# Mixed outputs of a hybrid encoder layer kept in two parts in HBM, their loads and those of w_out in a new order

## The chip, the cores and the metric

One core of one Trainium2 chip. The metric is the device time of one execution in microseconds (us). The times below are the median of three runs and one execution that was profiled.

## What is computed

One layer of a streaming encoder for 2048 prompt frames and 8 running streams of 16 frames. In the kernel these 2176 rows are 17 tiles of 128: tile 0 is the sample rows, tiles 1 to 16 are the prompt.

```
h = rms_norm(x, norm1_g);  p = h @ w_in                    # 1024 -> 3328
y_rw = rwkv7_mix(p[:, :1792])                              # 8 heads: chunked linear recurrence, group norm, gate
q, k, v = diff_project(p[:, 1792:])                        # rms norm and rope
o = softmax(q1 k1) v - lam * softmax(q2 k2) v              # chunk-causal; the samples with their cache
y_df = rms_norm(o, df_subln_g) * (1 - lam_init)
x = x + concat([y_rw, y_df]) @ w_out                       # the mixed outputs y: 1024 -> 1024
u = rms_norm(x, norm2_g) @ w_up                            # 1024 -> 5632
c = causal_dwconv(concat([conv_prev, u]), conv_w, conv_b)  # 3 taps
gate, up = split(c);  x = x + (silu(gate) * up) @ w_down   # 2816 -> 1024
```

Also written out are k, v, the last projected row, the recurrence's state and the last two rows of u. All is float32 to float32's precision: an operand is split into a high part rounded to the TensorE type (ACT copy, float32r) and a low part (DVE, value minus high), and a product is three matmuls: high x high, high x low, low x high.

## The kernel before, in words

The program is ordered by a planner (`Schedule`): every step of work is a Python generator (a stream) with a priority (0 is first); the planner has a model of each engine's time and always lets the stream go on whose operands it believes ready first and whose priority is lowest in number. What a stream issues goes, in that order, into the queues of the five engines, and each engine works its queue in order. All DMAs go through one queue, that of SP, which waits in order for what a transfer needs. `yield sd.has(...)` holds a stream until keys are done, `yield Slot(pool, tag)` until a buffer of a ring is free. Memory is handed out by hand (`Memory`, `Pool`), PSUM in 8 banks.

Three stages overlap at their edges. `phase_1`: q, k, v and the attention of the prompt; `subln` norms one pair of heads of a tile, turns it with TensorE and stores it in `scr["yt"]`, [feature / 128, 128, rows] float32 in HBM. `phase_2`: the rest of the projection (`project`, six blocks of tiles, each with 14 weight pieces that later blocks load from `s_wr`), the operands of the recurrence (`prep`, `prep2`). Beside what follows run `solver` (small triangular systems, DVE mostly), `chain` (the recurrence, tile by tile, each ended by `chain_out`, which norms, gates, turns and stores the other half of y), `samples` and `decode`.

`phase_3` works four blocks of four prompt tiles; the last has tile 0 too. It is set up when the key "projected" is done. Per block b: `inputs(b)` loads the block's mixed outputs Y: eight pieces of 128 x 512 go through a staging ring C of two buffers (shared with the convolutions), ACT makes the high part and DVE the low one in the tiles `hhi` and `hlo`. For b > 0 it waits for the keys ("up", b-1) and the last convolutions of block b-1; `hhi` and `hlo` are the very tiles that hold that block's normed h2, which the up units read. `out(b)` multiplies by w_out: a first half of 512 columns over four accumulators, then a second; `accumulate` adds each to the residual x (DVE), which frees the bank; `residuals` loads x only when the second stage is through (key "left"). `norm2` makes h2. Then 22 `up_unit`s (weights j and j + 22, the last one is unit 43), with five `down` groups between them (after j = 4, 8, 12, 16, 21), each two halves of columns; then `out(b+1)`, then the sixth `down` group. The key ("up", b) is set after the fifth group.

`order` lists the weight pieces in the order of use. The first time that a piece is used, `fetch` loads it raw (512 KB, ring `raw3` of two), `split` makes its two parts in the ring `w3` of four, and `keep` stores the parts (1 MB, `s_w3`, in the profile `s_w`); later blocks load the parts (1 MB). `weights` is allowed three pieces ahead of the one in use. The eight pieces of w_out have the numbers 66 to 73.

All instructions are recorded in one helper (L379 in the profile), so rows are told apart by operand names and shapes; tiles in SBUF are all named memory, PSUM is banks, `s_...` is scratch in HBM, `in_...` an input.

Of the kernel before, what the change touches and what calls it, by code (L numbers as in the profile page):

```python
# [462 lines left out]
class Kernel:  # L463
# [135 lines left out]
    def phase_1(self, scr, attention, scoring, projection):  # L599
# [376 lines left out]
        def values():  # L976

            q = 0
            for n in range(64):
# [12 lines left out]
                if h == 1:  # L992
                    yield
                    o = self.t(tp, [128, 256], "oB")
                    self.let(po)
                    for x in range(2):
                        nc.scalar.activation(o[:, x * 128:x * 128 + 128], po[:, x * 128:x * 128 + 128], AF.Identity, scale=rc.pop((p, i, x))[:, 0:1])
                    sd.add(self.subln(tp, mp, px, o, scr["yt"][4 + 2 * p:6 + 2 * p, :, (i + 1) * 128:(i + 2) * 128], "px"), 1, ("subln", p, i))
# [43 lines left out]
    def subln(self, tp, mp, pxt, o, dst, ptag):  # L1042
# [19 lines left out]
        yield  # L1062
        self.let(pt)
        yo = self.t(tp, [128, w], "sqB")
        nc.scalar.activation(yo, pt[:, :w], AF.Copy)
        yield
        nc.sync.dma_start(dst.rearrange("k p t -> p k t"), yo.rearrange("p (k t) -> p k t", k=H))


    def phase_2(self, scr, ctx, projection, early):  # L1070
# [3 lines left out]
        hp, xp, wr, wp = P("h2", 2), P("x2", 1), P("raw2", 2), P("w2", 3)  # L1074
# [119 lines left out]
        def weights():  # L1194
            for gi in range(nb * 14):
# [5 lines left out]
                if gi == 14:  # L1201
                    yield sd.has("scored", ("unit2", 13))
                    early.close()
                    sd.done.add("early")
# [462 lines left out]
    def chain_out(self, i, y, tiles, pools, tp, dst):  # L1667
# [44 lines left out]
        yo = self.t(t1, [128, 4, 128], "W")  # L1712
        nc.scalar.activation(yo, pt.rearrange("p (k t) -> p k t", k=4), AF.Copy)
        self.let(pt)
        yield
        nc.sync.dma_start(dst.rearrange("k p t -> p k t"), yo)
        yield "stored"

    def chain(self, scr, P, px):
# [13 lines left out]
        for i in range(1, NTILE):  # L1733
# [32 lines left out]
            yield from self.chain_out(i, y, tiles, pools, tp, scr["yt"][0:4, :, i * 128:i * 128 + 128])  # L1766
# [6 lines left out]
    def samples(self, scr, P, px):  # L1773
# [73 lines left out]
        yield from self.chain_out(0, y, tiles, pools, tp, scr["yt"][0:4, :, 0:128])  # L1847
        sd.done.add("samples")

    def decode(self, scr, P, px):  # L1850
# [118 lines left out]
        for x in range(2):  # L1969
            oh = self.t(tp, [128, 256], "oh")  # L1970
            nc.vector.tensor_copy(oh, o[:, x * 256:x * 256 + 256])
            yield from self.subln(lp, mp, px, oh, scr["yt"][4 + 2 * x:6 + 2 * x, :, 0:128], "px")
# [4 lines left out]
    def phase_3(self, scr, ctx):  # L1977
# [6 lines left out]
        wr = self.pools(rctx, True)("raw3", 2)  # L1984
# [47 lines left out]
        parts, made, used, known = {}, set(), [0], set()  # L2032
        first = [known.isdisjoint((x,)) and not known.add(x) for _, x in order]
# [12 lines left out]
        def fetch():  # L2046
            for i, (src, _) in enumerate(order):
# [9 lines left out]
        def weights():  # L2057
            for i in range(len(order)):
# [38 lines left out]
        def inputs(b):  # L2097
# [5 lines left out]
            if b:  # L2103
                yield sd.has(("up", b - 1), ("c", b - 1, 21), ("c", b - 1, 43))
            Y = [self.t(hp, [128, KT, NT], t, F32R, 128, KT * 640) for t in ("hhi", "hlo")]
            for k in range(KT):
                yield Slot(up, "C")
                raw = self.h(up, [128, NT], "C", room=640)
                runs = [(0, tiles[0], 4)] + ([(512, 0, 1)] if 0 in tiles else [])
                for o, i, n in runs:  # L2110
                    nc.sync.dma_start(raw[:, o:o + n * 128], yt[k, :, i * 128:(i + n) * 128])

                def done(k=k):
                    st["y"][k] = (Y[0][:, k], Y[1][:, k])

                sd.add(split(raw, Y[0][:, k], Y[1][:, k], done), 1)
            yield lambda: all(st["y"])
# [206 lines left out]
        def main():  # L2324
            yield from out(0)
            for b in range(nb):
# [17 lines left out]
        def all_inputs():  # L2344
            for b in range(nb):
# [9 lines left out]
    def run(self, scr):  # L2355
# [3 lines left out]
        with ExitStack() as ctx, ExitStack() as right, ExitStack() as left, ExitStack() as projection, ExitStack() as early:  # L2359
# [63 lines left out]
def lay_out(inputs):  # L2423
# [37 lines left out]
           "t": (NTILE, 4, 8, 32, 32), "yt": (KT, 128, NTILE * 128), "os": (128, 512), "xt": (NTILE, 128, D),  # L2461
# [43 lines left out]
```

## Time and profile before

| | us |
|---|---|
| time, median of 3 (lowest, highest) | 3441.08 (3439.51, 3445.29) |
| the profiled execution's own time | 3451.01 |
| its span, first to last instruction | 3448.8 |
| TensorE (PE) busy in the span | 3302.8 |
| VectorE (DVE) busy | 1977.7 |
| ScalarE (ACT) busy | 1391.5 |
| GpSimd (POOL) busy | 730.5 |
| HBM traffic, read and written | 514.00 MB, 181.09 MB |

How to read it: PE is the engine of the matmuls, PEld its weight loads, which overlap them. A row of a timeline gives start, duration, engine, operation, destination<-source, count, and in brackets the idle time of the engine just before and what ended it. Neighbouring instructions of a kind are merged in one row. SPq is the queue through which transfers are issued; its durations are the issuing, not the transfer. The granted clock (PEclk) is 1.00 at 2.4 GHz and 0.50 at 1.2 GHz.

### The profile page before, as it was taken

The numbers are of one execution on the slowest core, as the hardware profiler recorded it, in microseconds if no ns is written. First come the engines' busy times: TensorE is split into PE (matmuls) and PEld (weight loads), VectorE is DVE, ScalarE is ACT, GpSimd is POOL, SyncE is SP. The second block draws the span as 40 slices with busy tenths as digits, with TensorE's granted clock in tenths as the row PEclk, the third lists the DMA queues.
The fourth block names the chain that finished last, engine by engine and source line by source line (L and its number), as shares of the span: only waits on it lengthen the run. The fifth ranks groups of instructions, "written<-read, shape, count | busy, mean of one in ns | idle before, by whom it ended". The sixth has DMA issues, their size and how long they took to land.

```text
span 3448.8 us, 60191 instructions
## 1 busy us (share of the span) xinstructions
PE 3302.8 (96%) x23596; PEld 2753.1 (80%) x23596; DVE 1977.7 (57%) x3338; ACT 1391.5 (40%) x2837; POOL 730.5 (21%) x1700
## 2 busy tenths in 40 slices
PE   7999999988999997999999999999999999999999
PEld 6888788877888885777777777776667887899998
DVE  5787677786685657896664545435333333333334
ACT  5676566674444543434442322223232122222221
POOL 4433243333223321122211112131000000000000
PEclk9999999999999998999999999999999999999999
DMA  5433243178877777787785755657785565544443
GB/s 187 133 99 93 83 117 88 44 246 305 266 264 262 247 266 271 232 276 284 275 313 193 254 182 186 229 185 262 255 286 196 192 226 189 176 154 151 147 149 143
DMA packets 311099, 699.02 MB, mean 203 GB/s; under 512 B 124800, under 2 KB 198400, under 8 KB 260000
## 3 DMA queue, kind: packets, MB, share of 16 engines
q1 hardware_dynamic: 310816, 695.18, 59.1%
q8 instruction: 186, 3.05, 0.4%
q14 instruction: 97, 0.79, 0.1%
HBM read 514.00 MB, written 181.09 MB: 202 GB/s over the span
## 4 chain that ended last, share of the span: by engine, by line
PE 73%; DVE 11%; DMA 7%; issue 3%; POOL 2%; ACT 2%; SPq 1%; DVEq 0%; POOLq 0%; ACTq 0%
PE banks L379 73%; DVE memory L379 11%; POOL memory L379 2%; ACT memory L379 2%; SPq L379 1%; DMA memory<-s_xt 1%; DMA memory<-s_ar 1%; DMA memory<-s_yt 1%; DMA memory<-in_cv 0%; DMA s_wr<-memory 0%; DMA memory<-s_a 0%; DMA memory<-in_w_down 0%; DMA memory<-o_kp 0%; DMA s_tm<-memory 0%; DMA memory<-s_tm 0%
## 5 line engine op out<-in xcount | busy, mean ns | idle before, releaser
L379 PE MATMUL banks<-memory 128*128 128x512 f32 (+11 forms) x18952 | 2572.3, 309 | 64.4 <-ACT memory L379 31.1
L379 PEld LDWEIGHTS banks<-memory 128*128 128x128 f32 (+4 forms) x18824 | 2081.3, 164 | 446.4 <-issue 135.0
L379 ACT ACTIVATE memory<-banks 128x512 f32<-128x512 f32 (+8 forms) x1199 | 515.4, 442 | 1251.9 <-PE banks L379 1053.9
L379 DVE SCALAR_TENSOR_TENSOR memory<-memory 128x512 f32<-128x512 f32 (+7 forms) x830 | 605.0, 757 | 483.2 <-ACT memory L379 420.4
L379 ACT ACTIVATE memory<-memory 128x512 f32<-128x512 f32 (+11 forms) x921 | 618.3, 692 | 605.6 <-DVE memory L379 328.1
L379 PE MATMUL banks<-memory,memory 128*128 128x512 f32 (+3 forms) x3156 | 735.3, 368 | 10.2 <-DVE memory L379 5.0
L379 PEld LDWEIGHTS banks<-memory,memory 128*128 128x128 f32 (+1 forms) x3156 | 530.2, 188 | 117.1 <-DVE memory L379 12.4
L379 POOL COPY memory<-memory 128x2 f32<-128x2 f32 (+4 forms) x640 | 151.1, 261 | 1537.1 <-ACT memory L379 1500.7
L379 DVE TENSOR_TENSOR memory<-memory,memory 128x1024 fp32r<-128x1024 f32 (+6 forms) x289 | 280.7, 978 | 153.8 <-ACT memory L379 152.2
L379 DVE TENSOR_TENSOR memory<-memory 128x256 f32<-128x256 f32 (+18 forms) x501 | 290.1, 582 | 87.7 <-POOL memory L379 71.9
L379 DVE TENSOR_TENSOR memory<-memory,banks 128x512 f32<-128x512 f32 x238 | 162.1, 686 | 252.2 <-PE banks L379 250.9
L379 PE MATMUL banks<-ident,memory 128*128 128x128 f32 x1488 | 231.8, 282 | 67.3 <-DVE memory L379 32.5
L379 PEld LDWEIGHTS banks<-ident,memory 128*128 128x128 f32 x1488 | 177.3, 144 | 108.6 <-DVE memory L379 35.5
L379 POOL TENSOR_TENSOR memory<-memory 128x64 f32<-128x64 f32 (+6 forms) x453 | 216.1, 491 | 200.5 <-ACT memory L379 101.4
L379 DVE TENSOR_TENSOR memory<-banks,memory 128x256 f32<-128x256 f32 (+4 forms) x274 | 129.0, 471 | 209.2 <-PE banks L379 153.8
L379 ACT ACTIVATE memory<-banks,memory 128x128 f32<-128x128 f32 (+7 forms) x308 | 213.0, 706 | 85.2 <-DVE memory L379 56.2
L379 POOL TENSOR_TENSOR memory<-memory,mexp 128x4 f32<-128x4 f32 (+4 forms) x177 | 187.6, 1060 | 128.4 <-DVE memory L379 115.7
L379 DVE TENSOR_REDUCE memory<-banks 128x1 f32<-128x1024 f32 (+7 forms) x192 | 172.5, 908 | 36.1 <-PE banks L379 35.5
L379 DVE TENSOR_REDUCE memory<-memory 128x4 f32<-128x256 f32 (+24 forms) x314 | 145.1, 466 | 58.4 <-ACT memory L379 52.7
L379 POOL TENSOR_SCALAR memory<-memory 128x4 f32<-128x4 f32 (+4 forms) x159 | 44.3, 279 | 624.6 <-DVE memory L379 341.3
L379 ACT ACTIVATE memory<-banks,pvec 128x384 f32<-128x384 f32 (+1 forms) x98 | 49.3, 518 | 83.1 <-PE banks L379 77.6
L379 DVE SCALAR_TENSOR_TENSOR memory<-banks,memory,memory 128x384 f32<-128x384 f32 (+1 forms) x98 | 52.4, 537 | 52.6 <-ACT memory L379 50.6
(40 smaller groups left out, 465.8 us busy)
## 6 DMA issues: line engine op xcount, KB each, us to landing
memory<-s_w SPq DMA_DIRECT2D x222, 1024.0 KB
s_w<-memory SPq DMA_DIRECT2D x74, 1024.0 KB
memory<-s_wr SPq DMA_DIRECT2D x70, 1024.0 KB
memory<-in_w_up SPq DMA_DIRECT2D x44, 512.0 KB
memory<-s_xt SPq DMA_DIRECT2D x34, 512.0 KB
s_a<-memory SPq DMA_DIRECT2D x68, 256.0 KB
memory<-s_a SPq DMA_DIRECT2D x17, 1024.0 KB
memory<-in_x_prompt SPq DMA_DIRECT2D x32, 512.0 KB
```

The source lines that it names most:

```text
L379: r = f(*a, **k)
```

## The change

It does five things.

1. `scr["yt"]` gets a leading dimension of two: `subln` and `chain_out` (through the new `mixed`) make the high part with the ACT pass that they had, then a low part with a DVE subtraction from PSUM, and store both, with two DMAs.
2. `inputs` loads both parts straight into `hhi` and `hlo`, two 128-feature groups to a DMA, without ring C and without passes on ACT and DVE.
3. For b > 0 it waits for ("up", b-1) alone, and that key is set after the last up unit, ahead of the fifth `down` group.
4. `phase_3` is set up before "projected" is waited for; its weights, inputs and main part wait for that key themselves, but `fetch` already starts when five of the six blocks of the projection are done. Its raw ring is three deep and lies elsewhere; the second stage's raw ring is closed earlier.
5. w_out's pieces are loaded raw and split in the first two blocks, and stored in the second instead of the first.

```
-        hp, xp, wr, wp = P("h2", 2), P("x2", 1), P("raw2", 2), P("w2", 3)
+        hp, xp, wp = P("h2", 2), P("x2", 1), P("w2", 3)
+        rctx = ExitStack()
+        wr = self.pools(rctx, True)("raw2", 2)          # closed with early.close(), ahead of unit 14
...
+    def mixed(self, dst, p, hi, lo):
+        nc = self.nc
+        nc.scalar.activation(hi.bitcast(F32R), p, AF.Copy)
+        yield hi
+        nc.vector.tensor_tensor(out=lo.bitcast(F32R), in0=p, in1=hi, op=ALU.subtract)
+        yield lo
+        for x, part in enumerate((hi, lo)):
+            nc.sync.dma_start(dst[x].rearrange("k p t -> p k t"), part.rearrange("p (k t) -> p k t", t=128))
...
-        wr = self.pools(rctx, True)("raw3", 2)
+        wr = self.pools(rctx)("raw3", 3)
...
+        times = [sum(y == x for _, y in order[:i]) for i, (_, x) in enumerate(order)]
+        keeps = [n == (x >= 66) for n, (_, x) in zip(times, order)]
+        first = [n <= (x >= 66) for n, (_, x) in zip(times, order)]
...
         def fetch():
+            yield sd.has(("proj2", 4))
...
         def weights():
+            yield sd.has("projected")
...
-                    sd.add(keep(order[i][1], w), 1)
+                    if keeps[i]:
+                        sd.add(keep(order[i][1], w), 1)
...
             if b:
-                yield sd.has(("up", b - 1), ("c", b - 1, 21), ("c", b - 1, 43))
+                yield sd.has(("up", b - 1))
             Y = [self.t(hp, [128, KT, NT], t, F32R, 128, KT * 640) for t in ("hhi", "hlo")]
-            for k in range(KT):
-                yield Slot(up, "C")
-                raw = self.h(up, [128, NT], "C", room=640)
...
+            for k in range(0, KT, 2):
+                for x in range(2):
+                    for o, i, n in runs:
+                        nc.sync.dma_start(Y[x][:, k:k + 2, o:o + n * 128].bitcast(F32), yt[x, k:k + 2, :, i * 128:(i + n) * 128].rearrange("k p t -> p k t"))
+                for q in (k, k + 1):
+                    st["y"][q] = (Y[0][:, q], Y[1][:, q])
+                yield []
...
                     yield from up_unit(b, j)
+                    if j == 21:
+                        sd.done.add(("up", b))
                     if j in late(b):
                         yield from down(b, late(b)[j])
-                sd.done.add(("up", b))
...
+            self.phase_3(scr, ctx)
             sd.run(["projected"])
             projection.close()
             self.shut(self.middle[-1][1])
-            self.phase_3(scr, ctx)
```

## Rows read from the trace of the kernel before

**Rows 1.** The page: the span, and the busy time of each engine with its share of the span and its instructions.

```profile
span 3448.8 us, 60191 instructions
PE 3302.8 (96%) x23596; PEld 2753.1 (80%) x23596; DVE 1977.7 (57%) x3338; ACT 1391.5 (40%) x2837; POOL 730.5 (21%) x1700
```

**Rows 2.** The chain of waits that ended last, in order of time (start, duration, what): its pieces at the starts of blocks 1, 2 and 3.

```profile
1843.44 5.19 DMA memory<-s_yt
...
2387.84 7.40 DMA memory<-s_yt
...
2891.23 4.96 DMA memory<-s_yt
```

**Rows 3.** TensorE's timeline from 1316 to 1397 us, the start of block 0; the last row is out(0)'s last.

```profile
1324.25 0.79 PE L379 MATMUL banks<-memory 128*128 128x512 f32 x1 [8.34 <-ACT memory L379]
...
1330.67 3.62 PE L379 MATMUL banks<-memory 64*64 64x128 f32 x28
...
1337.97 0.43 PE L379 MATMUL banks<-memory 64*64 64x128 f32 x4 [3.35 <-ACT memory L379]
...
1339.68 6.36 PE L379 MATMUL banks<-memory 64*64 64x128 f32 x24 [1.28 <-DVE memory L379]
...
1346.30 4.08 PE L379 MATMUL banks<-memory 64*64 64x128 f32 x30
...
1359.36 1.22 PE L379 MATMUL banks<-memory 128*128 128x512 f32 x2 [2.52 <-ACT memory L379]
...
1366.46 21.73 PE L379 MATMUL banks<-memory 128*128 128x512 f32 x88 [5.87 <-DVE memory L379]
...
1394.57 2.33 PE L379 MATMUL banks<-memory 128*128 128x512 f32 x9
```

**Rows 4.** Windows of 10 us there: length, busy time (instructions) of PE, PEld, DVE, ACT and POOL, then the granted clock, the DMA engines' busy share, and GB/s.

```profile
1320.00:1330.00 10.00, 5.29 (x17) 4.00 (x18) 4.34 (x7) 2.12 (x2) 0.00 (x0) 0.57 0.53 131
...
1340.00:1350.00 10.00, 10.00 (x57) 7.62 (x49) 9.52 (x23) 3.21 (x6) 0.00 (x0) 0.71 1.02 414
...
1360.00:1370.00 10.00, 4.13 (x11) 2.82 (x10) 9.53 (x10) 1.06 (x1) 0.00 (x0) 0.52 1.00 383
```

**Rows 5.** TensorE's timeline at the starts of blocks 1, 2 and 3.

```profile
1847.87 1.11 PE L379 MATMUL banks<-ident,memory 128*128 128x128 f32 x4 [4.87 <-POOL memory L379]
...
2388.86 2.76 PE L379 MATMUL banks<-memory 128*128 128x64 f32 x18 [1.47 <-DVE memory L379]
...
2395.95 10.63 PE L379 MATMUL banks<-memory 128*128 128x512 f32 x80 [4.33 <-ACT memory L379]
...
2878.99 11.36 PE L379 MATMUL banks<-memory,memory 128*128 128x512 f32 x48
...
2897.07 43.28 PE L379 MATMUL banks<-memory 128*128 128x512 f32 x179 [6.71 <-ACT memory L379]
```

**Rows 6.** Windows of 5 us at these three places, columns as in rows 4.

```profile
1850.00:1855.00 5.00, 5.00 (x15) 3.93 (x14) 1.40 (x3) 1.44 (x3) 0.00 (x0) 0.57 0.54 157
...
2375.00:2380.00 5.00, 5.00 (x30) 3.23 (x32) 4.48 (x8) 1.19 (x3) 0.00 (x0) 1.00 1.00 365
...
2395.00:2400.00 5.00, 4.05 (x9) 2.77 (x9) 1.32 (x3) 1.88 (x3) 0.00 (x0) 0.50 0.38 122
...
2895.00:2900.00 5.00, 2.93 (x7) 2.19 (x8) 1.64 (x2) 1.48 (x2) 0.00 (x0) 0.54 0.50 164
...
2900.00:2905.00 5.00, 5.00 (x19) 4.01 (x18) 1.65 (x2) 1.48 (x2) 0.00 (x0) 0.78 0.48 138
```

**Rows 7.** The timeline of SP's queue: at the start of block 0, at one store of a mixed output (the fourth of chain_out after 1312, tile 8), and ahead of block 3.

```profile
1312.78 1.82 SPq L379 DMA_DIRECT2D memory<-s_yt  x2
...
1314.64 0.91 SPq L379 DMA_DIRECT2D memory<-in_w_out  x2
...
1316.54 13.79 SPq L379 DMA_DIRECT2D memory<-s_a  x16
...
1332.26 0.91 SPq L379 DMA_DIRECT2D s_w<-memory  x2
...
1357.28 3.10 SPq L379 DMA_DIRECT2D memory<-in_x_prompt  x4
...
1714.97 0.38 SPq L379 DMA_DIRECT2D s_yt<-memory  x1
...
2868.30 22.41 SPq L379 DMA_DIRECT2D memory<-s_w  x5
```

**Rows 8.** The timeline of ACT and DVE at the start of block 0: the first split of a w_out piece, the first split of a Y piece that had waited, and the first residual add.

```profile
1323.14 1.06 ACT L379 ACTIVATE memory<-memory 128x1024 fp32r<-128x1024 f32 x1 [4.74 <-DMA memory<-in_w_out]
...
1324.23 1.23 DVE L379 TENSOR_TENSOR memory<-memory,memory 128x1024 fp32r<-128x1024 f32 x1 [3.11 <-ACT memory L379]
...
1335.37 0.63 ACT L379 ACTIVATE memory<-memory 128x512 fp32r<-128x512 f32 x1 [9.82 <-DMA memory<-s_yt]
...
1336.03 0.69 DVE L379 TENSOR_TENSOR memory<-memory,memory 128x512 fp32r<-128x512 f32 x1 [5.87 <-ACT memory L379]
...
1368.57 0.69 DVE L379 TENSOR_TENSOR memory<-memory,banks 128x512 f32<-128x512 f32 x1 [0.43 <-PE banks L379]
```

**Rows 9.** What bears on the makers: the page's group of DVE operations from PSUM and memory (busy, mean ns of one, idle before); and the sum of TensorE's waits for DVE (total us, times, longest).

```profile
L379 DVE TENSOR_TENSOR memory<-banks,memory 128x256 f32<-128x256 f32 (+4 forms) x274 | 129.0, 471 | 209.2 <-PE banks L379 153.8
...
PE banks L379 <- DVE memory L379: 56.4, 44, 7.9
```

More of the change, by code (lines that the diff above doesn't have):

```diff
@@ L1062, in subln @@
         yield
+        hi, lo = self.t(tp, [128, w], "sqB"), self.t(tp, [128, w], "sqB")
+        yield from self.mixed(dst, pt[:, :w], hi, lo)
         self.let(pt)
[L1064 to L1067, printed above, removed]
+    def mixed(self, dst, p, hi, lo):
[6 more added lines that the diff above has]
+            nc.sync.dma_start(dst[x].rearrange("k p t -> p k t"), part.rearrange("p (k t) -> p k t", t=128))
     def phase_2(self, scr, ctx, projection, early):
@@ L1711, in chain_out @@
         yield pt
-        yo = self.t(t1, [128, 4, 128], "W")
-        nc.scalar.activation(yo, pt.rearrange("p (k t) -> p k t", k=4), AF.Copy)
+        hi, lo = self.t(t1, [128, 512], "W"), self.t(t1, [128, 512], "Ub")
+        yield from self.mixed(dst, pt, hi, lo)
         self.let(pt)
-        yield
-        nc.sync.dma_start(dst.rearrange("k p t -> p k t"), yo)
         yield "stored"
@@ L1765, in chain @@
                 yield from self.chain_chunk(c, tiles, pools, W, y, U, through, update)
-            yield from self.chain_out(i, y, tiles, pools, tp, scr["yt"][0:4, :, i * 128:i * 128 + 128])
+            yield from self.chain_out(i, y, tiles, pools, tp, scr["yt"][:, 0:4, :, i * 128:i * 128 + 128])
             sd.done.add(("chain", i))
@@ L1846, in samples @@
             nc.sync.dma_start(d["o_wkv"][:, f, 4 * c:4 * c + 4], S)
-        yield from self.chain_out(0, y, tiles, pools, tp, scr["yt"][0:4, :, 0:128])
+        yield from self.chain_out(0, y, tiles, pools, tp, scr["yt"][:, 0:4, :, 0:128])
         sd.done.add("samples")
@@ L1971, in decode @@
             nc.vector.tensor_copy(oh, o[:, x * 256:x * 256 + 256])
-            yield from self.subln(lp, mp, px, oh, scr["yt"][4 + 2 * x:6 + 2 * x, :, 0:128], "px")
+            yield from self.subln(lp, mp, px, oh, scr["yt"][:, 4 + 2 * x:6 + 2 * x, :, 0:128], "px")
         yield "stored"
@@ L2031, in phase_3 @@
             plan_down(5)
-        parts, made, used, known = {}, set(), [0], set()
-        first = [known.isdisjoint((x,)) and not known.add(x) for _, x in order]
+        parts, made, used = {}, set(), [0]
+        times = [sum(y == x for _, y in order[:i]) for i, (_, x) in enumerate(order)]
+        keeps = [n == (x >= 66) for n, (_, x) in zip(times, order)]
+        first = [n <= (x >= 66) for n, (_, x) in zip(times, order)]
         def split(raw, hi, lo, done):
@@ L2103, in inputs @@
             if b:
-                yield sd.has(("up", b - 1), ("c", b - 1, 21), ("c", b - 1, 43))
+                yield sd.has(("up", b - 1))
             Y = [self.t(hp, [128, KT, NT], t, F32R, 128, KT * 640) for t in ("hhi", "hlo")]
-            for k in range(KT):
-                yield Slot(up, "C")
-                raw = self.h(up, [128, NT], "C", room=640)
[L2109 to L2117, printed above, removed]
+            runs = [(0, tiles[0], 4)] + ([(512, 0, 1)] if 0 in tiles else [])
+            for k in range(0, KT, 2):
[5 more added lines that the diff above has]
+                yield []
         def residuals():
@@ L2324, in main @@
         def main():
+            yield sd.has("projected")
             yield from out(0)
@@ L2344, in all_inputs @@
         def all_inputs():
+            yield sd.has("projected")
             for b in range(nb):
```

5 lines of the change are left out of this document (3 added, 2 removed).

## The prediction

> **What bounds the kernel now.** I read the page first. TensorE is busy 3302.8 of 3448.8 us [rows 1], so nothing that leaves TensorE's order of work as it is can return more than the 146 us in which it sits idle, plus what is worked at the lower clock. The question is which part of that belongs to the change. The chain of waits in order of time answers it: from the third stage on it is TensorE nearly without a break, and where it isn't, the pieces at the starts of blocks 1 to 3 are transfers of the mixed outputs s_yt [rows 2]. So I read these four places in TensorE's timeline, then the clock and the DMA in short windows, then who holds SP, ACT and DVE there.
>
> Start of block 0: TensorE stops at 1315.9 and resumes at 1324.25; up to 1366.46 the gaps shown are 8.34, 3.35, 1.28, 2.52 and 5.87, together 21.4 us [rows 3]. All name ACT or DVE, but ACT itself waits for transfers (9.82 us for s_yt, 4.74 for w_out) [rows 8], and these were issued late: two s_yt and two w_out loads go out at 1312.78 to 1315.5, then the two-deep staging rings are full and sixteen small s_a loads of the solver hold SP for 13.79 us; w_out's stores come into the same queue from 1332.26 [rows 7]. In this stretch the granted clock is 0.57, 0.71 and 0.52 of full [rows 4]: a window at share c spent (1-c)/0.5 of itself at 1.2 GHz, so 8.6, 5.8 and 9.6 us. At most the busy 5.29, 5.8 and 4.13 us of these were worked at half speed, which loses half of 15.2, 7.6 us; I take 6 us, for the gaps take part of the low stretch. The place costs about 27 us.
>
> Starts of blocks 1 to 3: gaps of 4.87, then 1.47 and 4.33, then 6.71, together 17.4 us [rows 5]. Behind them the clock is at 0.57 for 5 us, 0.50 while 4.05 us are worked, 0.54 and 0.78 [rows 6]: 2.1, 2.0 and 2.5 us lost. So the three cost 7.0, 7.8 and 9.2 us, together 24.
>
> **The loads of the next block let in sooner, without staging.** At block 3 the last group of down before the gap is 48 matmuls in 11.36 us, 0.237 us each [rows 5]. Today the Y loads wait until that group is through; with the change they may go once unit 43 has read the old operands, 11.4 us earlier. Two 512 KB loads of w_out issued at 1314.64 were taken up by ACT at 1323.14, 8.5 us after [rows 7, 8]; the first pair of Y is also 1 MB and lands inside the 11.4 us even so. At 371 GB/s, a rate between those of two full windows (365 at 2375, 383 at 1360) [rows 4, 6], the 4.2 MB of a block take 11.3 us and a pair 2.8, against 24 x 0.237 = 5.7 us in which TensorE uses a pair. ACT's 0.63 us and DVE's 0.69 us per piece [rows 8] and the turn of the two-deep ring fall away. Block 3: all 9 us. Block 2: the DMA engines are full there with the decode's loads (share 1.00 [rows 6]) and Y now has 2.1 MB more, 5.7 us at 371 GB/s, bounds 0 (it starts earlier) and 5.7; I take 3, leaving 5. Block 1: the gap's releaser is POOL, in a chain_out tile that was put ahead of out(1) because Y was late [rows 5]; if it remains, only the clock and the small waits behind it come back, if not, 7; I take 5. Sum: -19 us (bounds -9 and -24).
>
> A wait is added: SP reaches a Y load and waits for TensorE to finish unit 43; the weight loads behind it wait too. Three weights ahead, of 5.7 us each, cover 17 us, more than the 11.3 us of the transfer. Nothing else in the order needs SP in that time but the decode's loads (block 2, above).
>
> The Trainium skill, "DMA: Bandwidth & Descriptors", section "Anatomy of one DMA", says that the DMA engines never wait for a semaphore, the issuing sequencer does, before it dispatches. The trace agrees: ahead of block 3 the issuing of five weight loads, which wait for their buffers, is spread over 22.41 us of SP [rows 7]. By it the whole queue stands behind a Y load, which speaks against letting them in sooner; it is the second rival, whose price follows from rows.
>
> **w_out asked for early, stored late.** Three of eight raw pieces are loaded while the projection's fifth block is still at work; the ring is three deep; the eight stores of 1 MB leave the start of block 0, where they were 8.4 MB / 371 GB/s = 22.6 us of DMA time, and SP no longer waits there for DVE's low part. At the start of block 1, 8 raw loads of 0.5 MB take the place of 8 of 1 MB (-11.3 us of DMA), the stores come there (+22.6 us) and 8 splits are added, 1.06 us of ACT and 1.23 us of DVE each [rows 8]. Per weight that is 1.57 MB / 371 GB/s = 4.2 us of DMA and 1.23 us of DVE against 5.7 us of TensorE: hidden. If that cover failed, each would show 2.3 us, 18 in all.
>
> Block 0 with the change: the first Y pair, issued near 1312.8, is there 8.5 us later, at 1321.3 (bound from above 1324.25, as now; from below 1318 by the 371 GB/s), and w_out is there already: 3 of the 8.34 us. Of the other 13.0 us, ACT's wait for s_yt and 8 x 0.69 = 5.5 us of DVE passes go; raw piece 3 still has to come behind the sixteen s_a loads (1316.5 + 13.8 = 1330.3, landing some 6 to 8 us later), while three pairs need 17 us and the projection's left-over work, three tiles of 3.6 to 4.1 us [rows 3], some 12, so TensorE asks for it at about 1350. I take 10 of the 13 (bounds 0 and 13). Of the 6 us of clock 4. Sum: -17 us. Condition: the second half of out(0) takes the PSUM banks of the first, and these are freed only by the residual adds, whose x loads went out at 1357.28 and whose first add ran at 1368.57 [rows 7, 8]. The x loads follow the last tiles of the second stage, and these tiles stood behind the same ACT wait of 9.82 us, so they move up too; if not, see the first rival.
>
> **Makers.** 34 calls of subln and 17 of chain_out (one store each today) get one DVE subtraction and one more store each. DVE from PSUM at 128x256 is about 0.47 us by its group [rows 9], at 128x512 0.69 by its nearest row: 34 x 0.47 + 17 x 0.69 = 27.7 us of DVE, 51 x 0.38 [rows 7] = 19 us of SP. Removed are 32 splits. No matmul waits for a maker, but a transpose bank is held longer and DVE's other work moves back. TensorE waited for DVE 44 times in the whole run, 56.4 us [rows 9]; from 0 to 27.7 us, and I take 3, near the lower end since DVE rarely is the last.
>
> **Sum.** -17 - 19 + 3 = -33 us on the profiled execution of 3451.0 us (span 3448.8, 2.2 us around it). The median shown, 3441.08, is 0.3% lower; the same 33 us give 3408.
>
> **Rivals.**
> 1. The start of block 0 gives its gain back: the residual adds stay where they are, or DVE, which is full behind it (9.53 of 10 us [rows 4]), sets the pace. Then out(0)'s first half ends at 1321.3 + 22.7 + 12 = 1356 and TensorE waits until about 1369; the second half ends 22.7 us later at 1392 instead of 1396.9 [rows 3]. Gain there 5 instead of 17: 3420. For it: the x loads are untouched by the change. Against: the ACT wait ahead of them goes.
> 2. The weights stand behind Y on SP. If only one weight is ahead in fact, each of the three starts waits 11.3 - 5.7 = 5.6 us: +17, 3425. Against: the ring holds four weights, and ahead of block 3 SP issued five weight loads before it came to Y [rows 7].
> 3. Everything is regained: 27 + 24 - 0: 3390.
> 4. The loads aren't let in sooner in effect, because the chain's tiles or the landing set them, and block 0 is rival 1 with its clock lost again: within 3434 to 3448, centre 3440. Against: the eighth prompt tile's store, the last that block 1 needs, is issued at 1714.97 [rows 7].
> 5. Slower: the makers. If TensorE, DVE's in-order queue between, waits for each subtraction and store, 51 x (0.69 + 0.38) = 55 us on top of the -36 of the rest: 3460. It decides from 0.84 us per maker on (43 us, slower by 7). For it: the first stage has only two transpose banks, which go in turn; against: 56.4 us is all that TensorE lost to DVE so far.
>
> **How the numbers follow.** Forecast 0.48, rival 1 0.17, rival 2 0.10, rival 3 0.05, rival 4 0.09, rival 5 0.11. A difference of 0.2%, 7 us, is about what a measurement of this kernel can tell from no change. Faster: 0.48 + 0.17 + 0.10 + 0.05 = 0.80; within 0.2%: 0.09; slower: 0.11. The forecast's own range is 3396 to 3420 (its bounds at block 0 and at the starts). The range of 8 in 10 goes from 3388, which takes in rival 3, to 3438, which takes in rivals 1 and 2 and half of 4.
>
> **What would show it.** Right: the three s_yt pieces are gone from the chain of waits; no gap over 2 us ahead of the first out matmuls of blocks 1 to 3 and a clock of 1.00 there; no ACT or DVE pass from s_yt; out(0) done by about 1380 and no s_w store before it; TensorE's busy time in the first 1300 us within 5 us of now. Wrong: a gap of over 5 us in mid out(0) that an add ends (rival 1); TensorE waiting for s_w behind Y (2); the start of block 0 later than 1312 by more than 10 us, with more DVE releasers in the first stage (5). What I can't see is the new order: the instructions of all engines are ordered by a planner with its own model of time, and shifted by a few us it may place filler differently everywhere; that is the width of the forecast's range.

## The result, and the profile after

The changed kernel takes 3406.38 us (median of 6 runs, 3401.21 to 3426.02) against 3445.19 (6 runs, 3439.51 to 3450.12): ratio 0.990, 95% interval 0.9879 to 0.9922. The profiled execution is the longest of the six, 3426.02 us with a span of 3424.2, so the two traces lie only 24.6 us apart where the medians lie 38.8. The page begins:

```profile
span 3424.2 us, 60364 instructions
...
PE 3297.0 (96%) x23596; PEld 2750.6 (80%) x23596; DVE 1983.1 (58%) x3365; ACT 1376.9 (40%) x2813; POOL 735.7 (21%) x1700
```

TensorE is busy as long as before, within 6 us [rows 1]: what went is mostly idle time, 127.2 us of the span instead of 146.0. In the chain of waits of after one s_yt load is left, at the start of block 0; the three pieces of [rows 2] are gone:

```profile
1314.89 4.63 DMA memory<-s_yt
```

**Starts of blocks 1 to 3.** TensorE's timeline there. Rows from `memory,memory` belong to the fifth `down` group of the block that ends, those from `memory` alone to the work behind it:

```profile
1823.69 36.50 PE L379 MATMUL banks<-memory 128*128 128x512 f32 x177
...
2352.98 17.23 PE L379 MATMUL banks<-memory 128*128 128x512 f32 x150
...
2863.87 11.36 PE L379 MATMUL banks<-memory,memory 128*128 128x512 f32 x48
2875.07 41.68 PE L379 MATMUL banks<-memory 128*128 128x512 f32 x183
```

No bracket of idle time stands in any of them, where [rows 5] had 4.87, 1.47 and 4.33, and 6.71 us. SP's queue ahead of block 3 shows why: the sixteen s_yt loads go out 0.6 us after that last group of 48 began, not when it is through:

```profile
2836.85 27.53 SPq L379 DMA_DIRECT2D memory<-s_w  x6
2864.43 12.75 SPq L379 DMA_DIRECT2D memory<-s_yt  x16
...
2878.16 17.86 SPq L379 DMA_DIRECT2D memory<-s_w  x5
```

Windows of 5 us (columns as in [rows 4]): the first is behind the start of block 1, the other two on either side of block 3's first matmul. The granted clock is 1.00 in all, and at block 2 from 2350 to 2360 us too, where [rows 6] had 0.50 to 0.78 behind the gaps:

```profile
1825.00:1830.00 5.00, 5.00 (x24) 4.14 (x23) 4.32 (x7) 0.88 (x1) 0.00 (x0) 1.00 1.04 412
...
2870.00:2875.00 5.00, 5.00 (x23) 4.04 (x22) 3.52 (x6) 0.00 (x0) 0.00 (x0) 1.00 1.07 373
2875.00:2880.00 5.00, 5.00 (x24) 4.10 (x23) 0.69 (x1) 0.00 (x0) 0.00 (x0) 1.00 1.08 362
```

**Start of block 0.** TensorE's timeline from the projection's end to the first up unit (compare [rows 3]):

```profile
1315.99 0.55 PE L379 MATMUL banks<-ident,memory 128*128 128x128 f32 x3 [1.56 <-ACT memory L379]
1318.19 5.79 PE L379 MATMUL banks<-memory 128*128 128x512 f32 x12 [1.66 <-DMA memory<-s_yt]
...
1342.31 13.89 PE L379 MATMUL banks<-memory 128*128 128x512 f32 x60 [0.29 <-DVE memory L379]
1358.18 8.23 PE L379 MATMUL banks<-memory 128*128 128x512 f32 x35 [1.97 <-DVE memory L379]
1372.47 1.12 PE L379 MATMUL banks<-ident,memory 128*128 128x128 f32 x4 [6.07 <-DVE memory L379]
...
1379.44 2.32 PE L379 MATMUL banks<-memory 128*128 128x512 f32 x9
1381.60 1.03 PE L379 MATMUL banks<-ident,memory 128*128 128x128 f32 x8
1390.52 1.97 PE L379 MATMUL banks<-ident,memory 128*128 128x128 f32 x8 [7.89 <-DVE memory L379]
1394.25 1.97 PE L379 MATMUL banks<-ident,memory 128*128 128x128 f32 x8 [1.76 <-DVE memory L379]
1396.05 25.27 PE L379 MATMUL banks<-memory 128*128 128x512 f32 x104
```

The waits for ACT and loads ahead of out(0), 8.34 and 3.35 us in [rows 3], have become 1.56 and 1.66, and out(0) is done at 1381.8 (before 1396.9). But then TensorE waits for DVE: 6.07 us in mid out(0), 7.89 and 1.76 ahead of the transposes for the first up unit. All three waits end at transposes of `norm2` (the rows x4 and x8 from `ident,memory`). DVE's timeline ahead of the first of them shows what DVE does: the residual adds (the `banks` row) and `norm2`'s own pass (the last row, behind POOL) stand between passes of the solver over 128x1024, 1.2 to 1.9 us each, and in the window behind them DVE is busy for the whole 10.00 us while TensorE works 2.63:

```profile
1366.46 1.93 DVE L379 TENSOR_TENSOR memory<-memory 128x1024 f32<-128x1024 f32 x1
1368.30 1.29 DVE L379 TENSOR_TENSOR memory<-memory,banks 128x512 f32<-128x512 f32 x2
1369.49 1.22 DVE L379 TENSOR_REDUCE memory<-memory 128x64 f32<-128x1024 f32 x1
1371.13 1.29 DVE L379 SCALAR_TENSOR_TENSOR memory<-memory 128x1024 f32<-128x1024 f32 x1 [0.42 <-POOL memory L379]
```

```profile
1380.00:1390.00 10.00, 2.63 (x16) 2.05 (x14) 10.00 (x10) 6.34 (x9) 0.88 (x3) 0.75 0.42 139
```

**Where the time went.** The measure used below is the issue of block 0's first Y load, called T0 (the projection is done there), and the time from T0 to the end of the span; both are read from SP's timeline and the span. It leaves out one source of spread: T0 itself differs by 12 us between two executions of the same changed kernel (1314.46 and 1302.47), while the rest agrees within 6. It does not leave out the planner: another order of the changed kernel's very operations (the row "another order") is 8.5 and 14.6 us shorter from T0 on than the changed kernel's two executions. A single difference of that size in the last column therefore does not by itself show what a part is worth:

```
kernel                     T0        T0 to first Y load of block 1, 2, 3    T0 to end
before                     1312.78   530.7   1075.1   1578.0                2136.0
before, again              1307.88   526.4   1071.1   1569.3                2127.6
after                      1314.46   496.5   1022.3   1550.0                2109.7
after, again               1302.47   497.2   1021.9   1543.9                2103.7
loads let in late          1311.30   501.5   1037.1   1565.9                2124.3
stored in block 0          1301.93   521.1   1047.4   1549.6                2109.5
w_out asked for late       1301.91   511.0   1045.7   1553.4                2113.2
stored in 0, asked late    1307.40   504.4   1025.0   1550.4                2110.2
all three undone           1305.86   516.4   1049.4   1574.5                2132.8
makers alone               1303.03   517.5   1065.2   1569.3                2126.8
another order              1306.11   492.5   1012.8   1535.4                2095.2
solver held                1301.93   493.5   1023.5   1548.0                2107.8
solver early               1324.56   516.5   1054.6   1522.0                2081.7
```

Before takes 2131.8 us from T0 on (mean of two), after 2106.7: -25. The last column is the one to compare: in the three between, a Y load let in sooner is itself some 11 us earlier, and filler work done in one block is missing in another.

### The profile page after: what moved, and what is told of

Read it like the earlier page. It is cut to its first block, busy times and chain, and to the rows that moved or that the text cites. A ratio compares the mean times of both kernels' runs of the same rounds, so it can differ in the third digit from the quotient of the medians.

```text
span 3424.2 us, 60364 instructions
## 1 busy us (share of the span) xinstructions
PE 3297.0 (96%) x23596; PEld 2750.6 (80%) x23596; DVE 1983.1 (58%) x3365; ACT 1376.9 (40%) x2813; POOL 735.7 (21%) x1700
## 4 chain that ended last, share of the span: by engine, by line
PE 73%; DVE 10%; DMA 8%; issue 3%; ACT 3%; POOL 3%; SPq 1%; DVEq 0%; ACTq 0%; POOLq 0%
PE banks L379 73%; DVE memory L379 10%; ACT memory L379 3%; POOL memory L379 2%; DMA s_tm<-memory 1%; SPq L379 1%; DMA memory<-s_a 1%; DMA memory<-in_w_up 1%; DMA memory<-s_wr 1%; DMA memory<-s_tm 1%; DMA s_g<-memory 1%; DMA memory<-o_vs 0%; DMA memory<-in_x_prompt 0%; DMA memory<-s_ar 0%; DMA memory<-o_kp 0%
## 5 line engine op out<-in xcount | busy, mean ns | idle before, releaser
L379 PE MATMUL banks<-memory 128*128 128x512 f32 (+9 forms) x19000 | 2566.5, 308 | 37.5 <-DVE memory L379 15.0
L379 ACT ACTIVATE memory<-banks 128x512 f32<-128x512 f32 (+9 forms) x1199 | 515.0, 441 | 1218.3 <-PE banks L379 990.7
L379 ACT ACTIVATE memory<-memory 128x512 f32<-128x512 f32 (+10 forms) x897 | 605.7, 695 | 634.9 <-DVE memory L379 405.3
L379 PE MATMUL banks<-memory,memory 128*128 128x512 f32 (+3 forms) x3108 | 721.9, 374 | 9.1 <-DVE memory L379 9.0
L379 PEld LDWEIGHTS banks<-memory,memory 128*128 128x128 f32 (+1 forms) x3108 | 519.9, 187 | 117.2 <-DVE memory L379 13.2
L379 DVE TENSOR_TENSOR memory<-memory 128x256 f32<-128x256 f32 (+19 forms) x491 | 283.0, 579 | 100.1 <-POOL memory L379 82.6
L379 DVE TENSOR_TENSOR memory<-banks,memory 128x256 f32<-128x256 f32 (+5 forms) x325 | 155.1, 477 | 210.4 <-PE banks L379 159.0
L379 PEld LDWEIGHTS banks<-ident,memory 128*128 128x128 f32 x1488 | 179.3, 145 | 119.9 <-DVE memory L379 45.2
L379 POOL TENSOR_TENSOR memory<-memory 128x64 f32<-128x64 f32 (+6 forms) x463 | 225.7, 503 | 225.0 <-ACT memory L379 110.1
L379 POOL TENSOR_TENSOR memory<-memory,mexp 128x4 f32<-128x4 f32 (+4 forms) x177 | 186.8, 1056 | 158.8 <-DVE memory L379 146.0
L379 DVE TENSOR_REDUCE memory<-banks 128x1 f32<-128x1024 f32 (+7 forms) x192 | 172.6, 907 | 25.8 <-PE banks L379 24.2
L379 DVE TENSOR_REDUCE memory<-memory 128x4 f32<-128x256 f32 (+23 forms) x314 | 145.1, 465 | 43.7 <-ACT memory L379 38.6
L379 DVE COPY_PREDICATED memory<-memory,banks 128x256 f32<-128x256 int32 x136 | 52.8, 440 | 54.3 <-PE banks L379 46.5
L379 DVE SCALAR_TENSOR_TENSOR memory<-banks,memory,memory 128x384 f32<-128x384 f32 (+1 forms) x98 | 52.2, 536 | 55.2 <-ACT memory L379 49.3
```

The costliest lines, as they stand in the source:

```text
L379: r = f(*a, **k)
```

## The experiments

Theories: (A) the prediction's: the Y loads going out sooner take the gaps at the starts of blocks 1 to 3, w_out's early load and late store and the direct loads take idle time at the start of block 0, the makers cost little. (B) Its rival 1: DVE gives the gain at block 0 back. (C) All of it is a new order by the planner, and no part has a price of its own. Each ratio is set against executions of the kernel before that were taken beside it; their medians are 3439.67 us (first four experiments), 3439.79 (the kernel before again, all three undone, makers alone, solver held), 3441.91 (another order, solver early, makers twice) and 3441.95 (the last).

**The changed kernel again.**

> The changed kernel once more, beside the three that each undo one of its parts. Expected 3406 us as measured, and a profile nearer to it than the first one (3426 us). Theory (the removed waits are the gain): no gap over 2 us at the starts of blocks 1 to 3 in this execution too. Rival (the new order of all instructions is the gain): the gaps at other places differ from the first profile by as much as the gain.

3411.51 us, ratio 0.9917 (0.9897 to 0.9938). The two measurements put the effect at 39 and 28 us.

**Loads let in late.** The Y loads wait for the fifth `down` group and the last convolutions again, still direct and in two parts:

```
-                yield sd.has(("up", b - 1))
+                yield sd.has(("up", b - 1), ("c", b - 1, 21), ("c", b - 1, 43))
...
-                    if j == 21:
-                        sd.done.add(("up", b))
...
+                sd.done.add(("up", b))
```

> The Y loads wait again for the fifth down group and the last convolutions, all else as changed. Theory: a gap of 4 to 6 us returns at the starts of blocks 1, 2 and 3 (the first pair of Y lands some 5.5 us after it is issued), with 2 us of lower clock behind each: 15 to 24 us slower than the changed kernel, about 3425 us. Rival 1 (the passes on ACT and DVE were the wait, not the moment of issue): at most 5 us slower. Rival 2 (order alone): anything within 10 us either way, without gaps at these places.

3424.09 us, ratio 0.9959 (0.9943 to 0.9975): 12.6 more than the changed kernel beside it, and from T0 to the end 15 to 21 us more. Gaps of 3.88 and 1.53 us are back at block 2, but hardly one at block 1 (0.62 us), though 4 to 6 were expected at each: there the loads still go out at 1812.76, some 6 us before the group's last row. The gap at block 3 is back, and the clock behind it falls (TensorE's timeline, then windows of 5 us):

```profile
2865.43 11.36 PE L379 MATMUL banks<-memory,memory 128*128 128x512 f32 x48
2883.12 1.19 PE L379 MATMUL banks<-memory 128*128 128x512 f32 x2 [6.33 <-DMA memory<-s_yt]
2884.82 43.28 PE L379 MATMUL banks<-memory 128*128 128x512 f32 x181 [0.51 <-DMA memory<-s_yt]
```

```profile
2875.00:2880.00 5.00, 1.79 (x8) 1.13 (x6) 1.38 (x2) 0.00 (x0) 0.00 (x0) 0.87 0.48 152
2880.00:2885.00 5.00, 1.37 (x3) 0.68 (x4) 0.00 (x0) 0.00 (x0) 0.00 (x0) 0.50 1.03 377
2885.00:2890.00 5.00, 5.00 (x14) 3.95 (x15) 0.00 (x0) 0.00 (x0) 0.00 (x0) 0.60 1.07 364
```

The gap, 6.33 and 0.51 us, is as long as the 6.71 of before [rows 5], though no ACT or DVE pass is left in it: its releaser is now the transfer itself. From the end of the fifth `down` group to the end of the span it is 558.8 us here (3435.6 - 2876.79), 558.5 before (3448.8 - 2890.35 [rows 5]) and 549.0 after (3424.2 - 2875.23). The makers alone, whose loads also come late, have 557.8; the changed kernel again and every run below with the sooner loads have 548.9 to 549.1, whatever their order. So the start of block 3 is worth 9.5 us, and all of it comes from when the loads may go.

**w_out stored in block 0** (pieces stored when they are first loaded, as before):

```
-        keeps = [n == (x >= 66) for n, (_, x) in zip(times, order)]
-        first = [n <= (x >= 66) for n, (_, x) in zip(times, order)]
+        keeps = [n == 0 for n, (_, x) in zip(times, order)]
+        first = [n == 0 for n, (_, x) in zip(times, order)]
```

> w_out's parts are stored in the first block again and loaded as parts in the second, all else as changed. Theory: eight stores of 1 MB come back into the start of block 0 (22.6 us of DMA at 371 GB/s) and hold SP for DVE's low part; out(0) ends 5 to 8 us later: 3412 us. Rival (the DMA time there is covered and the store's place is neutral): within 3 us of the changed kernel.

3414.23 us, ratio 0.993 (0.9915 to 0.9945), 2.7 more than the changed kernel: not to be told from none.

**w_out asked for late.**

```
-            yield sd.has(("proj2", 4))
+            yield sd.has("projected")
```

> w_out is asked for only when the projection is done, all else as changed. Theory: the first three raw pieces land some 8 us after they are asked for, behind the Y loads in SP's queue: the first matmul of out(0) waits for a split until about 1326 instead of 1318, and the whole is 6 to 9 us slower: 3414 us. Rival (the start of block 0 is bounded by the residual adds and the solver's DVE work, so an earlier first half is waited off later): within 3 us.

3412.66 us, ratio 0.9923 (0.9908 to 0.9939), 1.2 more than the changed kernel. TensorE's timeline at the start of block 0 does show what the early load is for:

```profile
1329.65 0.79 PE L379 MATMUL banks<-memory 128*128 128x512 f32 x1 [14.88 <-ACT memory L379]
```

Idle in the 110 us from T0 is 35.5 us here, 37.4 with the store in block 0, and 22.7 and 23.8 in the two executions of after. But those 12 to 15 us don't arrive at the end: from T0 to the end both kernels lie within 7 us of after's mean. Over the whole stretch from T0 TensorE idles 55.2 us here, 53.1 with the store in block 0, and 52.5 and 45.2 in after. An idle stretch in one block that other blocks make good is not a price.

**The kernel before again.**

> The kernel before once more, for a second profile of it and for the width of a comparison of equal kernels. Every theory: ratio 1.000 within 0.002; the gaps at the starts of blocks 0 to 3 as in the first profile within 2 us each. What is open: whether the moment at which the projection is done (1312.8 us in the first profile) differs between executions by ten us, as it did between two of the changed kernel (1314.5 and 1302.5).

3437.09 us, ratio 0.9996 (0.9986 to 1.0006): two builds of one kernel agree within 0.1%.

**All three undone**: late let-in, early store and late asking together. What is left of the change is that the makers store two parts, that these are loaded without passes, and that the raw ring is three deep and the third stage set up earlier.

> The mixed outputs in two parts, loaded straight into the operand tiles; but the loads wait as in the kernel before, and w_out is asked for when the projection is done and stored in the first block. Theory (the parts add up): slower than the changed kernel by what the three undone parts showed, 12.6 + 2.7 + 1.2 = 16 us, so about 3425 us, some 14 us faster than before. Rival (what the direct loads give depends on their coming sooner): within 5 us of the kernel before.

3439.15 us, ratio 0.9997 (0.9988 to 1.0006); 2132.8 us from T0 to the end, before's own mean being 2131.8. The two parts, without the new order, bring nothing. Nor do the three prices add up: by the medians they are 12.6, 2.7 and 1.2 us one by one, some 16, but 28 when all three are undone together. Part of the difference is block 1, where a gap of 6.27 us is back that the late loads alone did not bring. Block 3's start:

```profile
2868.56 11.36 PE L379 MATMUL banks<-memory,memory 128*128 128x512 f32 x48
2886.26 1.19 PE L379 MATMUL banks<-memory 128*128 128x512 f32 x2 [6.34 <-DMA memory<-s_yt]
```

The gap is as long as before without the passes on ACT and DVE. That the doubled bytes have taken their place is likely, but no run separates the two.

**Makers alone.** The kernel before, whose makers make and store both parts; only the high part is loaded, through ring C and the split as before, so the low part that the makers store is left out of the products:

```
-            yield from self.chain_out(i, y, tiles, pools, tp, scr["yt"][0:4, :, i * 128:i * 128 + 128])
+            yield from self.chain_out(i, y, tiles, pools, tp, scr["yt"][:, 0:4, :, i * 128:i * 128 + 128])
...
-                    nc.sync.dma_start(raw[:, o:o + n * 128], yt[k, :, i * 128:(i + n) * 128])
+                    nc.sync.dma_start(raw[:, o:o + n * 128], yt[0, k, :, i * 128:(i + n) * 128])
```

> The kernel before, whose makers make and store both parts; its blocks load the high part alone through the staging ring and split it as before, so the low part is left out of the mixed outputs' product. Theory: the 51 more DVE subtractions and stores cost 3 us, at most 28: 3443 us. Rival (the makers' own rival of the prediction): 1.07 us for each, 55 us: 3495 us. Third possibility: no change within 0.2%, since DVE releases TensorE in few of its waits.

3431.82 us, ratio 0.9975 (0.9963 to 0.9988): no cost of the makers shows; the kernel is 8 us shorter with them. Added work can't do that by itself, so presumably the order moved: block 1's gap of 4.9 us, for one, is not there (no wait over 1.9 us). TensorE waits for DVE more often than in the kernel before again, 55 times and 69.7 us against 43 and 58.3, but not in the first 1300 us, where most makers stand (35.1 us against 36.0), and its idle time in all is the same, 131 and 130 us.

**Solver held.** In after, the solver's groups that the planner may put beside the start of block 0 also wait until block 0's four tiles are through `norm2` (the keys ("h", 0, j)), to get DVE free there:

```
-            yield sd.has(..., *["projected"] * (last > 1))
+            yield sd.has(..., *(["projected"] + [("h", 0, j) for j in range(4)]) * (last > 1))
```

> The changed kernel, in which the solver's three later groups begin only when block 0's norm2 is through, not when the projection is. Theory (what is left at the start of block 0 is the solver's 1 to 2 us DVE passes ahead of norm2 and its sixteen loads on SP): the gaps of 6.1, 7.9 and 1.8 us ahead of the first up unit shrink to 4 us in all, and the whole is 10 to 15 us faster than the changed kernel: 3396 us. Rival (DVE is full for 200 us behind, so the solver's work comes back as a wait later): within 4 us of the changed kernel, with new gaps from 1400 to 1600 us.

3411.51 us, ratio 0.9924 (0.9912 to 0.9936). Idle in the 110 us from T0 falls to 10.1 us, so it is the solver on DVE that TensorE waits for there. The end doesn't move (2107.8 us from T0, after 2106.7), for the chain is later too: the store of the last tile that block 1 needs goes out at 1792.47 (in after 1741.91), with the Y loads right behind it, and TensorE waits for them (SP's queue, then TensorE):

```profile
1792.47 1.15 SPq L379 DMA_DIRECT2D s_yt<-memory  x2
1795.40 4.58 SPq L379 DMA_DIRECT2D memory<-s_yt  x8
```

```profile
1790.65 1.11 PE L379 MATMUL banks<-ident,memory 128*128 128x128 f32 x4 [8.08 <-POOL memory L379]
1799.15 56.01 PE L379 MATMUL banks<-memory 128*128 128x512 f32 x491 [7.39 <-DMA memory<-s_yt]
```

**Another order.** In after, the planner's rate for DMAs is 350 instead of 360, which changes no operation, only its order:

```
-DMA_RATE = 360.0
+DMA_RATE = 350.0
```

> The changed kernel with one number of the planner's time model shifted (the rate at which it believes transfers run, 350 instead of 360), so that the work and its waits are the same and the order of instructions is another. It measures what a shift of order alone moves. Theory: at most 6 us either way from the changed kernel (3410 us), no gap at the starts of blocks 1 to 3. Rival (order is the gain): over 10 us either way.

3403.1 us, ratio 0.9886 (0.9867 to 0.9904), on a median 8 us under the changed kernel run again and 3 under its first measurement, the intervals overlapping. That is 7 us under the 3410 of the expectation, between its theory (6 at most) and its rival (over 10). No gap stands at the starts of blocks 1 to 3. From T0 to the end it is 2095.2 us, less than either execution of after, with 40.8 us of idle time against 52.5 and 45.2. The windows of the first 760 us, before, after and here, show what the order alone does to TensorE's busy time there:

```profile
0.00:760.00 760.00, 708.71 (x4650) 615.20 (x4651) 565.04 (x997) 498.80 (x1131) 279.06 (x638) 0.99 0.39 116
```

```profile
0.00:760.00 760.00, 711.76 (x4699) 618.29 (x4700) 579.83 (x1049) 502.56 (x1141) 283.39 (x652) 0.99 0.43 128
```

```profile
0.00:760.00 760.00, 720.19 (x4778) 623.83 (x4779) 583.94 (x1059) 506.76 (x1156) 291.46 (x658) 0.99 0.42 129
```

The whole change moves it from 708.71 to 711.76 us (the kernel before again has 710.44), this edit of a single planner value on to 720.19; the second execution of after has 714.38.

**Solver early.** In after, the solver's group for tiles 5 to 8 may start in the projection already:

```
-            yield sd.has(..., *["projected"] * (last > 1))
+            yield sd.has(..., *["projected"] * (last > 3))
```

> The changed kernel, in which the solver's group for tiles 5 to 8 may begin as soon as its operands are stored, inside the projection, instead of when the projection is done; the two groups after it are as they were. Theory (the start of block 0 is paced by that group's DVE passes and its sixteen loads on SP, and holding it back only made tile 8 late): TensorE's idle time in the 110 us after the projection falls from 23 to about 12 us without a gap at block 1: 10 us faster than the changed kernel, 3400 us. Rival (the sixteen loads then hold SP ahead of the projection's weight loads, 1 MB each 5 us): the gap moves ahead of the projection's end, within 4 us of the changed kernel.

3405.86 us, ratio 0.9894 (0.9875 to 0.9913), within the spread of after; idle in the 110 us from T0 is 26.8 us, not the 12 expected. T0 is 10 to 22 us later and the stretch behind it 22 to 28 us shorter: work changed its place and the sum stayed.

**Makers twice.** In after, each low part is made twice:

```
-        nc.vector.tensor_tensor(out=lo.bitcast(F32R), in0=p, in1=hi, op=ALU.subtract)
+        for _ in range(2):
+            nc.vector.tensor_tensor(out=lo.bitcast(F32R), in0=p, in1=hi, op=ALU.subtract)
```

> The changed kernel, in which each of the 51 makers makes its low part twice (the same DVE subtraction again, into the same place). It adds what the change added to DVE there once more: 34 x 0.47 + 17 x 0.69 = 27.7 us of DVE. Theory after the run with the makers alone (8 us faster, not slower): no cost, within 4 us of the changed kernel. Rival (the subtractions do cost, 3 us or more, and a luckier order hid it): 3 to 28 us slower.

3391.83 us, ratio 0.986 (0.9838 to 0.9881), with T0 at 1293.4, 9 to 21 us sooner than in after. This kernel no longer computes the layer: its first output is off by a relative 0.17, and why a repeated subtraction does that is not known. So its time prices nothing, and nothing below rests on this run.

**w_out as before, loads let in sooner** (the two edits of w_out undone together):

> The changed kernel with both changes to w_out undone: asked for when the projection is done, stored in the first block; the mixed outputs in two parts and their sooner loads are kept. Theory (the parts add up from the end of the projection on, where each run's profile shows them: 17.6 us for the sooner loads, 2.8 for the store, 6.5 for the asking): 9 us slower than the changed kernel from the end of the projection to the end, median about 3417 us. Rival (asking and storing only move idle time that DVE imposes anyway): within 4 us of the changed kernel. Second rival (each alone covers for the other, which would explain why the three undone together lost all the gain): 15 us or more slower.

3417.0 us, ratio 0.9927 (0.9916 to 0.9939); 2110.2 us from T0 to the end, after's mean being 2106.7. The expected 9 us more for the two edits is not there, nor the 15 or more of the second rival: it is 3.5 from T0, and 3 and 9 by the medians (ratios 0.9917 and 0.9900 for the changed kernel). Against all three undone (2132.8) the only edit that differs is the sooner loads: -22.6 us, whatever they shift in the order included.

## Why the prediction was right, and where it was not

The total was right: -33 us predicted; the two measurements of the changed kernel give -39 and -28. Theory A holds for the starts of blocks 1 to 3, B for the start of block 0, and C for the first two stages and for the small parts. The terms:

- **Starts of blocks 1 to 3, -19 us predicted: -23 measured** (all three undone to w_out as before; -15 to -21 from loads let in late to after). This is more than the 8.5 to 14.6 us that another order moves the same stretch, and block 3's share, 9.5 us where 9 were predicted, is the same in every order. The three gaps, 18.5 us together with all three undone, and the clock behind them are gone as foreseen. The mechanism was half right. The step "ACT's 0.63 us and DVE's 0.69 us per piece and the turn of the two-deep ring fall away" brought nothing: with late loads the gap is 6.33 and 0.51 us against 6.71. What counts is the moment of the issue. Whether the two parts are needed for that (without ring C and its passes the loads have only the old operands to wait for) was not tried by itself.
- **Rival 2, weights behind Y: refuted at block 3.** SP was in the s_yt loads for 12.75 us and came to the next weights at 2878.16, and TensorE has no gap up to 2916.
- **Start of block 0, -17 us predicted: -3.5 to -8.5 measured**, by undoing w_out's two edits (2110.2 against after's 2106.7 with the sooner loads, 2132.8 against 2124.3 with late ones); the direct loads alone, all three undone, bring nothing (2132.8 against 2131.8). This is the step that failed. Up to the end of out(0) it went as forecast: from T0 to there 84.1 and 79.5 us in the two executions of before, 67.3 in both of after, and 1381.8 for the forecast "about 1380". The x loads and the adds moved up, as the prediction's condition asked (issued at 1347.01, first add at 1351.71). Then most of it was given back by the second half of rival 1: DVE sets the pace, not in the adds but in `norm2`, whose passes stand behind the solver's. Windows of 110 us from T0 and of the 190 us behind, before and then after:

```profile
1312.78:1422.78 110.00, 79.86 (x454) 61.91 (x453) 84.78 (x138) 36.52 (x60) 9.98 (x20) 0.83 0.89 289
1422.78:1612.78 190.00, 185.47 (x1395) 145.64 (x1395) 161.62 (x215) 77.10 (x115) 39.60 (x62) 1.00 0.79 274
```

```profile
1314.46:1424.46 110.00, 87.30 (x429) 69.04 (x430) 79.98 (x123) 34.43 (x53) 13.62 (x23) 0.88 0.72 215
1424.46:1614.46 190.00, 178.33 (x1297) 140.68 (x1296) 168.13 (x223) 78.61 (x116) 34.37 (x64) 1.00 0.84 285
```

  TensorE's idle time in the 110 us went from 30.1 and 24.6 us (two executions) to 22.7 and 23.8, and in the 190 us from 4.5 and 3.9 to 11.7 and 7.4. The sum of both is as large as before; what remains is the clock: by its granted share, worked out as in the prediction, the 110 us hold 26.4 and 24.2 us at the lower level instead of 37.4 and 35.2. Ahead of the transposes for the first up unit TensorE waited 4.45 us before and 7.89 and 1.76 after. I had seen that DVE was full there [rows 4] and put that into a rival, instead of asking in the term itself what DVE had to do next. Storing early alone costs 2.8 us from T0 to the end and asking late alone 6.5. All these prices lie inside what another order moves (8.5 and 14.6 us), so what w_out's early asking and late storing are worth stays open, down to nothing.
- **Makers, +3 us predicted: not to be told from nothing.** In the changed kernel TensorE waited for DVE 46 times and 65.9 us, against 44 times and 56.4 [rows 9]; in the first 1300 us it is 35.8 us against 34.1, behind them 30.1 against 22.3. The second executions lie closer, 60.8 us in the changed kernel and 58.3 in the one before. The row of the changed kernel:

```profile
PE banks L379 <- DVE memory L379: 65.9, 46, 8.0
```

  T0 lies at 1306.0 on the mean of the table's eight rows from "after" to "makers alone" (1301.91 to 1314.46), and at 1310.3 in the two executions of before. Rival 5, 55 us on the path, is refuted by the makers alone.
- **The sum** came right in part by luck: block 0 brought some 8 to 13 us less than forecast, while the starts of the blocks may have brought 4 more, the makers took none of their 3, and T0 came 2 us sooner on the mean of two executions each, which is within its spread. By the profiled executions, two of each kernel, the whole is -27 us; the medians spread around that with the order and the execution.

What stays open: why the first two stages of one program take 1302 us once and 1314 another time, and how much of a change of 3 to 8 us in them is the change's at all. The predicted cause of the width, a planner that "may place filler differently everywhere" when it is shifted by a few us, is seen in the other order: no operation changed, and TensorE's work in the first 760 us moved by 6 to 8 us (the medians by 3 to 8, with intervals that overlap).

## What to carry to other kernels

Where a stage's loads wait for the last reader of a buffer, look first at which key lets them go: here, at block 3, some 11 us sooner took a gap of 6.8 us and some 3 us at the lower clock behind it, and removing all passes from the load without that took nothing. Idle time that goes at one place is a gain only if the next thing in line is ready: price the engine that is full behind the gap (here DVE at 10.00 of 10 us) in the term, not as a rival. And where a planner orders everything, run kernels that change its order alone, and believe no part whose price is less than what they move, unless it shows at one place in every order, as block 3's start does.

## What the runs showed that I had not expected

- With full DMA windows I had worked with 371 GB/s; the window at 1825 of after, fully busy as well, moves 412 GB/s, those around the s_yt loads of block 3 362 to 373.
- Two profiled executions of the changed kernel, taken apart, differ by 12 us in their first 1300 us and by 6 us in the 2100 behind; the six times of its first measurement go from 3401 to 3426 us.
- The granted clock is already at 0.50 in the window 2880 to 2885 of the kernel with late loads, in which TensorE worked 1.37 us, and 0.60 in the next, in which it worked all 5.00: a gap of 6.8 us cost 9.8 us in all (558.8 against 549.0).
